# VectorE in place of GpSimd for weight splits and additions, and a smaller scratch for the distance biases, in a one-core three-layer kernel

## The chip, the core and the metric

The kernel runs on one core of a Trainium2 chip. The metric is the device time of one execution in microseconds (us): all 26 inputs lie in device memory before it starts, and the output lies there when it ends. Lower is better.

## What is computed

The input x holds 256 rows of 1024 numbers, all in fp32. Three layers run one after another; the sizes are those that matter here.

```
h = rmsnorm(x, g0); p = h @ ev_w_in (1024 x 5120)
y = concat(hgrn2_scan(...) * silu(gate), retention_scan(rope(q), rope(k), v) * silu(gate)) @ ev_w_out (1536 x 1024)
x = x + rmsnorm(y, g1);  x = x + rmsnorm(square(relu(rmsnorm(x, g2) @ w1)) @ w2, g3)      # w1 1024 x 4096, w2 4096 x 1024

h = rmsnorm(x, g0); p = h @ od_w_in (1024 x 3080)
y = (sigmoid(og) * head_rmsnorm(mlstm_scan(q, k, v, gates))) @ od_w_out (1024 x 1024)
x = x + rmsnorm(y, g1);  x = x + rmsnorm(square(relu(rmsnorm(x, g2) @ w1)) @ w2, g3)

shift, scale, gate = split(silu(c) @ w_ada + b_ada)
h = rmsnorm(x, g) * (1 + scale) + shift; q, k, v, g_attn, cb, cc, cx, g_conv, m_attn, m_conv = split(h @ w_in (1024 x 10240))
attn: softmax(q k^T / sqrt(128) + bias[head, t5_bucket(t - s)], causal) v, 8 heads of 128
y = sigmoid(m_attn) * ((attn * silu(g_attn)) @ w_o_attn) + sigmoid(m_conv) * ((cb * conv3(cc * cx) * silu(g_conv)) @ w_o_conv)
out = rmsnorm(x + gate * (y @ w_out), final_g)
```

Almost all of the arithmetic is in the products of 256 rows with the weight matrices.

## The kernel before

**Weights.** All weights are fp32 and are read once, in units of 128 x 1024 numbers (512 KB). A unit is loaded on SyncE's queue into one of five buffers `raw` (`emit_load` L359, `load` L305). `emit_split` (L375) then makes two fp32r halves of it in one of eight buffers `u`: ScalarE copies it to the high half, and the low half is the unit minus that high half, one TENSOR_TENSOR of 128x1024 on VectorE or on GpSimd. L385 to L387 choose between the two by the finishing times that the planner expects, with POOL_BIAS (L33) as a handicap for GpSimd; 19 of the 316 splits went to GpSimd. A product is three fp32r matmuls per tile, high x high, high x low and low x high (`mmA` L445 with 512 columns a matmul, `mmB` L451 with 256), so TensorE needs both halves of a unit.

**Activations.** The 256 rows are two tiles T of 128 rows. Before a product they are transposed in 128x128 blocks on TensorE (`to_act` L542, the transposes are the lines `ax<-ident,s` at L296), ScalarE copies the result to a high part `a` (`a<-ax`), and VectorE subtracts to get the low part (`a<-ax,a`).

**Order.** The program `prog` is a list of units and small functions, laid out by stage builders: `blockA` (L464), `stagA` (L481: tile T = 0 over two column blocks, then T = 1), `blockB` (L501: output transposed). `Sched` (L48) keeps an estimated clock for each engine (a ScalarE, v VectorE, g GpSimd, p TensorE) and an estimated ready time for each tile, from cost formulas such as the one in `tt` (L263). Work beside the products is written as jobs, generators that wake when the estimated clock of TensorE reaches the time at which their inputs are expected. After each unit `pump` (L395) emits loads and splits as far ahead as buffers allow; a split due later than LEAD (7000 ns) waits until L406 and L407 find the engines free. So a change of one engine's estimate moves the order of instructions on every engine. Each engine then runs its instructions in that order, waiting by semaphores.

**Between products.** At the end of a mixer or MLP, `out_stag` (L606) starts `chain` (L580) for each T: `post` (L570) computes the rms factor and twice, for halves h of 512 columns, `s<-mm,sm,s` (SCALAR_TENSOR_TENSOR, L276) and x += s, the first half on GpSimd, the second on VectorE; `pre` (L551) makes the normalised input of the next product, two L276 lines `s<-x,sm,s`, then `to_act`. In layer 3 `pre` also adds a shift (`s<-s,s`, L265 on VectorE).

**First mixer.** `rope_evac` (L880) rotates q and k: three VectorE products and an addition of 128x512 on GpSimd (L893), then transposes. `ev_first` (L723) evicts v and the gate; the gate's product with `ghg` is done by GpSimd (L736).

**Second mixer (mLSTM).** `od_gates` (L1133) ends in `spread` (L1171): the row `ig` is written to a scratch `scr_m` in device memory and read back to 128 partitions, both on SyncE's queue. `mix_out` (L1293) computes for each T and pair of heads i numerator, denominator and head norm with small operations on 128x1 and 128x2 columns (`sm`), and writes y by two L276 lines. `od_og` (L1215) multiplies y by the sigmoid of the output gate (`s<-s,s`, L265 on VectorE) and calls `to_act`; the product with od_w_out follows.

**Distance biases.** `bias_rows` (L644) computes in the first MLP, early in the kernel, one row of 384 biases per head (8 partitions), and writes it to a scratch `scr` of [8, 128, 384] in device memory, the same row 128 times, on SyncE's queue. `bias_job` (L1436) reads it in layer 3 with a row pitch of 383, so that partition p sees its row shifted by p: 128 partitions x 8 heads x 256 numbers. The loads of weights before and after stand in the same queue.

GpSimd executes 44 instructions: 19 splits, 8 additions to x, 4 of rope, 2 products with `ghg`, and 11 memsets.

Of the kernel before, what the change touches and what calls it, by code (L numbers as in the profile page):

```python
# [10 lines left out]
F32 = mybir.dt.float32  # L11
# [3 lines left out]
ALU = mybir.AluOpType  # L15
# [14 lines left out]
SPREAD = 4000.0  # L30
MARGIN = 400.0
LEAD = 7000.0
POOL_BIAS = -200.0  # L33


LAST = -1.0
# [167 lines left out]
def tile_model(ctx: ExitStack, tc: tile.TileContext, I: dict, out: bass.AP, stop=None):  # L204
    nc = tc.nc
    sc = Sched()
# [4 lines left out]
    dram = ctx.enter_context(tc.tile_pool(name="scratch", bufs=1, space=bass.MemoryType.DRAM))  # L211
# [4 lines left out]
    def nm(p):  # L216
        cnt[0] += 1
        return f"{p}{cnt[0]}"

    def a8(dt=F32):  # L220
        return pool.tile([128, 2048], dt, tag="a8", bufs=6, name=nm("a8_"))

    def s4(dt=F32, n=1024):
        return pool.tile([128, n], dt, tag="s4", bufs=10, name=nm("s4_"))

    def s2(dt=F32, n=512):
        return pool.tile([128, n], dt, tag="s2", bufs=8, name=nm("s2_"))
# [9 lines left out]
    def axb():  # L237
        t = psum.tile([128, 512], F32, tag="ax", bufs=4, name=nm("ax_"))
        sc.reuse("ax", 4, t)
        return t  # L240


    def fs(ap):
        n = 1
        for s in ap.shape[1:]:
            n *= s
        return n
# [4 lines left out]
    def A(o, i, f=AF.Copy, **kw):  # L252
        c = fs(i) / 1.2 + 90
        ptr = [kw[k] for k in ("bias", "scale") if isap(kw.get(k))]
        acc = [kw["accum_out"]] if isap(kw.get("accum_out")) else []
        c += 93 * len(ptr) + 93 * len(acc)
        if f in TABLES and TABLES[f] != sc.table:
            sc.table = TABLES[f]
            c += 1283
        sc.op("a", c, [o] + acc, [i] + ptr)  # L260
        nc.scalar.activation(o, i, f, **kw)  # L261

    def tt(o, a, b, op, e="v"):  # L263
        sc.op(e, fs(o) * (1.0417 if e == "v" else 2.1) + 70, [o], [a, b])
        (nc.vector if e == "v" else nc.gpsimd).tensor_tensor(out=o, in0=a, in1=b, op=op)  # L265
# [8 lines left out]
    def stt(o, a, s, b, op0, op1, **kw):  # L274
        sc.op("v", fs(o) * 1.0417 + 70 + (60 if isap(s) else 0), [o], [a, b] + ([s] if isap(s) else []))
        nc.vector.scalar_tensor_tensor(out=o, in0=a, scalar=s, in1=b, op0=op0, op1=op1, **kw)  # L276
# [13 lines left out]
    def mm(o, l, r, start, stop_, c):  # L290
        sc.op("p", c, [o], [l, r])
        nc.tensor.matmul(o, l, r, start=start, stop=stop_)  # L292

    def tr(o, i, idt, c=107.0):
        sc.op("p", c, [o], [i, idt])
        nc.tensor.transpose(o, i, idt)  # L296
# [4 lines left out]
    def bc(ap2, n):  # L301

        return ap2[:, None, :].to_broadcast([ap2.shape[0], n, ap2.shape[1]])

    def load(o, i, q=None):  # L305
        sc.came(o, max(sc.E["p"], 0.0) + 4000.0)
        (q or nc.sync).dma_start(o, i)


    x = cpool.tile([128, 2, D], F32, name="x")  # L310
# [48 lines left out]
    def emit_load():  # L359
        k = st["load"]  # L360
        kind, val = order[k]
        t = pool.tile([128, 1024], F32, tag="raw", bufs=RB, name=nm("raw_"))
        src = units[val] if kind == "w" else val[0]
        if len(src.shape) == 3:
            load(t.rearrange("p (a c) -> p a c", a=src.shape[1]), src)
        else:
            load(t, src)
        raws[k] = t
        free = st["done"][k - RB] if k >= RB else 0.0
        st["dma"] = max(st["dma"], free + 2000.0) + 1480.0  # L370
        st["arrive"].append(st["dma"])
        sc.W[t.tensor.name] = [(0, 1024, st["dma"], "d")]
        st["load"] += 1

    def emit_split():  # L375
        k = st["split"]
        kind, val = order[k]
        t = raws.pop(k)
        if kind == "w":
            u = pool.tile([128, 2, 1024], F32R, tag="u", bufs=NU, name=nm("u_"))  # L380
            if len(st["free"]) >= st["nu"] - NU + 1 > 0:
                sc.W[u.tensor.name] = [(0, 2048, st["free"][st["nu"] - NU], "p")]
            st["nu"] += 1
            A(u[:, 0, :], t)
            hi_t = sc.E["a"] + sc.OTHER  # L385
            fv, fg = max(sc.E["v"], hi_t) + 1137.0, max(sc.E["g"], hi_t) + 2220.0
            tt(u[:, 1, :], t, u[:, 0, :].bitcast(F32), ALU.subtract, "g" if fg < fv + POOL_BIAS else "v")  # L387
            tiles[val] = u
            st["live"] += 1
        else:  # L390
            val[1](t)
        st["done"].append(max(sc.E["v"], sc.E["a"] + 1300.0))
        st["split"] += 1

    def pump():  # L395
        while True:
            k = st["split"]
            if st["load"] < len(order) and st["load"] < k + RB:
                emit_load()
                continue  # L400
            if k >= len(order):
                return
            if order[k][0] == "w" and st["live"] >= NU:
                return
            if order[k][0] == "w" and due[order[k][1]] - st["at"] > LEAD:
                if st["arrive"][k] > sc.t + 300 or sc.E["a"] > sc.t + 800 or \  # L406
                        min(sc.E["v"], sc.E["g"] + 1100.0) > sc.t + 500:  # L407
                    return
            elif st["arrive"][k] > sc.t + 1500:
                return  # L410
            emit_split()
# [158 lines left out]
    def post(T, st_, yb, g):  # L570

        rs = st_.second(yb[1])
        for h in range(2):
            c = slice(h * 512, h * 512 + 512)
            t = s2()
            stt(t, yb[h], rs, g[:, c], ALU.mult, ALU.mult)
            tt(x[:, T, c], x[:, T, c], t, ALU.add, "g" if h == 0 else "v")
        yield

    def chain(T, st_, yb, gpost, gpre, act, shift=None):  # L580
# [53 lines left out]
    E3 = {}  # L634
# [9 lines left out]
    def bias_rows():  # L644
        oh, rb, bm = E3["oh"], E3["rb"], E3["bm"]
        pb = axb()
        mm(pb[0:8, 0:384], rb[0:32, 0:8], oh[0:32, :], True, True, 640.0)
        tt(bm[0:8, :], pb[0:8, 0:384], bm[0:8, :], ALU.add)
        yield 1000.0
        scr = E3["scr"] = dram.tile([8, 128, 384], F32, name="scr")  # L650
        load(scr, bm[0:8, None, :].to_broadcast([8, 128, 384]))
        yield LAST


# [68 lines left out]
    def ev_first(T, b, ps):  # L723
        if T == 0:
            E1["vg", b] = s4()
            if b == SMALL:
                small_loads()
        if b == 0:
            v = E1["vg", 0][:, T * 512:T * 512 + 512]
            A(v, ps)  # L730
            E1["v", T] = v
        else:
            s_ = E1["vg", 1][:, T * 512:T * 512 + 512]
            A(s_, ps, AF.Sigmoid)
            tt(s_, ps, s_, ALU.mult)
            tt(s_.rearrange("p (h c) -> p h c", h=4), s_.rearrange("p (h c) -> p h c", h=4), bc(ghg, 4),  # L736
               ALU.mult, "g")
            E1["g", T] = s_
        if T == 1 and b == 0:
            sc.start(vec_job())  # L740

    stagA([(w_ev, 1024), (w_ev, 1536)], h0.get, ev_first, h0.before)

    def ev_f(ps):
# [135 lines left out]
    def rope_evac(key):  # L880
        def evac(ps):
            def job():
                dst = s4()
                E1[key] = dst
                for T in range(2):
                    p3 = ps[T].rearrange("p (h c) -> p h c", h=4)
                    m1, m2 = s2(), s2()
                    a3, b3 = (m.rearrange("p (h c) -> p h c", h=4) for m in (m1, m2))
                    cs, sn = (E1[k][:, T * 128:T * 128 + 128] for k in ("cos", "sin"))
                    tt(a3, p3, bc(cs, 4), ALU.mult)  # L890
                    tt(b3[:, :, 0:64], p3[:, :, 64:128], bc(sn[:, 0:64], 4), ALU.mult)
                    tt(b3[:, :, 64:128], p3[:, :, 0:64], bc(sn[:, 64:128], 4), ALU.mult)
                    tt(m1, m1, m2, ALU.add, "g")  # L893
                    yield
                    pt = axb()
                    for h in range(4):
                        tr(pt[:, h * 128:h * 128 + 128], m1[:, h * 128:h * 128 + 128], ident)
                    A(dst[:, T * 512:T * 512 + 512], pt)
                yield LAST
            E1[key + "job"] = sc.start(job())  # L900
        return evac
# [436 lines left out]
    m1 = Stage()  # L1338
# [97 lines left out]
    def bias_job():  # L1436
        scr = E3["scr"]
        E3["bias"] = a8().rearrange("p (h c) -> p h c", h=8)
        load(E3["bias"], bass.AP(tensor=scr.tensor, offset=scr.offset + 127,
                                 ap=[[383, 128], [128 * 384, 8], [1, 256]]))  # L1440
        yield LAST

    def silu_fm(ps, dst):
# [338 lines left out]
```

## Time and profile before

| | |
|---|---|
| three runs | 1004.68, 1004.59, 1003.57 us; median 1004.59 |
| the profiled execution | 1004.45 us |
| span of its trace, first to last instruction | 1002.6 us, mean granted TensorE clock 0.991 |
| busy TensorE / VectorE / ScalarE / GpSimd | 974.5 / 678.7 / 540.6 / 70.8 us |
| memory traffic | 187.46 MB read, 2.63 MB written |

The profile's times are microseconds from the span's start. PE is TensorE, DVE VectorE, ACT ScalarE, POOL GpSimd, SP SyncE. L265 is line 265 of the kernel; `out<-in` names tiles without their numbers (`mm` and `ax` are PSUM banks, `s` half or full working tiles, `sm` small columns). An idle time in brackets is that of the engine just before the instruction, with what ended it. PEclk is the TensorE clock that was granted, 1.00 being 2.4 GHz and 0.50 being 1.2 GHz.

### The profile page before, as it was taken

What the parts mean: (1) busy time and instruction counts of PE and PEld (TensorE: products, weight loads), DVE (VectorE), ACT (ScalarE), POOL (GpSimd) and SP (SyncE); (2) the same over time, 40 slices, a digit from 0 to 9 for tenths busy, and PEclk for the clock granted to TensorE, in tenths of its full rate; (3) what the DMA queues carried; (4) which work ended last, traced back from release to release, by engine and by line L of the source; (5) the groups of instructions that cost most, each with busy time, mean ns of one, the idle gap of its engine ahead of it and who ended that gap; (6) DMA issues with size and microseconds to landing.
All of it is one profiled execution on the core that took longest, in us unless ns stands there. A gap on an engine that the chain in (4) does not pass through costs nothing.

```text
span 1002.6 us, 15544 instructions
## 1 busy us (share of the span) xinstructions
PE 974.5 (97%) x6168; PEld 879.6 (88%) x6168; DVE 678.7 (68%) x852; ACT 540.6 (54%) x772; POOL 70.8 (7%) x44
## 2 busy tenths in 40 slices
PE   8999999999999899997999999999999999999997
PEld 6988888789989787986789999987999999999995
DVE  6769874875553367788698778658645677447564
ACT  7753674764542366766565545546545546444533
POOL 0212200200000001101201001001000010001000
PEclk9999999999999999998999999999999999999999
DMA  8762536566765666635489988635865445665631
GB/s 313 247 219 84 169 126 189 164 193 190 231 191 104 177 216 193 200 130 183 134 284 315 339 299 275 187 86 176 289 199 160 142 127 169 215 185 175 195 113 42
DMA packets 85100, 191.09 MB, mean 191 GB/s; under 512 B 7072, under 2 KB 10400, under 8 KB 85028
## 3 DMA queue, kind: packets, MB, share of 16 engines
q1 hardware_dynamic: 84740, 189.58, 59.8%
q8 instruction: 48, 0.79, 0.3%
q10 hardware_dynamic: 288, 0.52, 0.1%
q14 instruction: 24, 0.20, 0.1%
HBM read 187.46 MB, written 2.63 MB: 190 GB/s over the span
## 4 chain that ended last, share of the span: by engine, by line
PE 41%; issue 7%; DVE 2%; POOL 0%; ACT 0%; DVEq 0%; POOLq 0%
PE mm L292 35%; PE ax L292 6%; PE ax L296 1%; DVE s L265 1%; DVE u L265 0%; DVE s L276 0%; POOL u L265 0%; DVE s L271 0%; DVE x L265 0%; ACT junk L261 0%; POOL x L265 0%; ACT s L261 0%; DVE a L265 0%; ACT u L261 0%; DVE sm L280 0%
## 5 line engine op out<-in xcount | busy, mean ns | idle before, releaser
L265 DVE TENSOR_TENSOR u<-raw,u 128x1024 fp32r<-128x1024 f32 x297 | 368.0, 1253 | 212.1 <-ACT u L261 208.7
L261 ACT ACTIVATE u<-raw 128x1024 fp32r<-128x1024 f32 x316 | 329.9, 1056 | 276.6 <-PE mm L292 142.9
L292 PE MATMUL mm<-u,a 128*128 128x512 f32 x1968 | 473.4, 396 | 4.2 <-DVE a L265 3.2
L292 PEld LDWEIGHTS mm<-u,a 128*128 128x128 f32 x1968 | 368.3, 190 | 82.4 <-DVE a L265 4.6
L292 PE MATMUL mm<-a,u 128*128 128x256 f32 x2496 | 305.3, 284 | 0.0
L292 PEld LDWEIGHTS mm<-a,u 128*128 128x128 f32 x2496 | 301.5, 192 | 0.6
L292 PE MATMUL ax<-a,u 128*128 128x256 f32 x1152 | 142.4, 285 | 3.6 <-ACT u L261 2.9
L292 PEld LDWEIGHTS ax<-a,u 128*128 128x128 f32 x1152 | 141.3, 193 | 5.0 <-ACT u L261 3.1
L265 POOL TENSOR_TENSOR u<-raw,u 128x1024 fp32r<-128x1024 f32 x19 | 47.9, 2526 | 457.9 <-ACT u L261 332.0
L280 DVE RECIPROCAL sm<-sm 128x1 f32<-128x1 f32 (+2 forms) x43 | 7.0, 163 | 53.1 <-ACT sm L261 44.4
L296 PE MATMUL ax<-ident,s 128*128 128x128 f32 (+1 forms) x196 | 30.4, 275 | 11.2 <-DVE s L265 7.3
L261 ACT ACTIVATE s<-mm 128x512 f32<-128x512 f32 x64 | 35.6, 588 | 10.4 <-PE mm L292 10.1
L296 PEld LDWEIGHTS ax<-ident,s 128*128 128x128 f32 (+1 forms) x196 | 22.7, 140 | 19.4 <-issue 6.7
L261 ACT ACTIVATE a<-s 128x512 fp32r<-128x512 f32 (+1 forms) x37 | 23.8, 644 | 28.9 <-DVE s L265 28.1
L261 ACT ACTIVATE s<-ax 128x512 f32<-128x512 f32 (+1 forms) x43 | 24.3, 566 | 25.3 <-PE ax L296 13.9
L261 ACT ACT_TABLE_LOAD x27 | 34.6, 1283 | 2.0 <-DVE lbv L265 0.9
L265 DVE TENSOR_TENSOR s<-mm,s 128x512 f32<-128x512 f32 (+1 forms) x46 | 27.7, 638 | 10.8 <-PE mm L292 6.8
L265 POOL TENSOR_TENSOR x<-x,s 128x512 f32<-128x512 f32 x8 | 10.3, 1290 | 343.7 <-DVE s L276 343.7
L261 ACT ACTIVATE a<-ax 128x512 fp32r<-128x512 f32 x38 | 22.2, 592 | 22.0 <-PE ax L296 21.4
L265 DVE TENSOR_TENSOR a<-s,a 128x512 fp32r<-128x512 f32 x36 | 24.9, 693 | 11.2 <-ACT a L261 8.4
L265 DVE TENSOR_TENSOR s<-s,s 128x512 f32<-128x512 f32 (+4 forms) x38 | 30.4, 803 | 2.6 <-ACT s L261 1.9
L292 PE MATMUL ax<-s,s 128*128 128x256 f32 (+2 forms) x156 | 30.7, 338 | 0.8 <-DVE s L276 0.8
(101 smaller groups left out, 432.8 us busy)
## 6 DMA issues: line engine op xcount, KB each, us to landing
raw<-in_mlp_w_dram SPq DMA_DIRECT2D x128, 512.0 KB
raw<-in_w_in_dram SPq DMA_DIRECT2D x80, 512.0 KB
raw<-in_ev_w_in_dram SPq DMA_DIRECT2D x40, 512.0 KB
raw<-in_od_w_in_dram SPq DMA_DIRECT2D x24, 512.0 KB
raw<-in_w_ada_dram SPq DMA_DIRECT2D x24, 512.0 KB
raw<-in_ev_w_out_dram SPq DMA_DIRECT2D x12, 512.0 KB
s<-in_norm_g_dram SPq DMA_DIRECT2D x8, 512.0 KB
raw<-in_od_w_out_dram SPq DMA_DIRECT2D x8, 512.0 KB
```

Of the source, the lines that this page charges most:

```text
L261: nc.scalar.activation(o, i, f, **kw)
L265: (nc.vector if e == "v" else nc.gpsimd).tensor_tensor(out=o, in0=a, in1=b, op=op)
L280: nc.vector.reciprocal(o, i)
L292: nc.tensor.matmul(o, l, r, start=start, stop=stop_)
L296: nc.tensor.transpose(o, i, idt)
```

## The change

Every `tensor_tensor` that could go to GpSimd goes to VectorE: the low halves of all weight splits, the first half of x += s in `post`, the rope addition and the product with `ghg`. `pump` looks at VectorE's estimate alone. The planner's estimates change with that, and so does the order. The bias scratch holds each row 16 times instead of 128 times; it is read back by eight loads, each for 16 partitions, whose offset goes back by 16 numbers from one load to the next, so that each partition gets the same numbers as before.

```diff
-POOL_BIAS = -200.0
...
             A(u[:, 0, :], t)
-            hi_t = sc.E["a"] + sc.OTHER
-            fv, fg = max(sc.E["v"], hi_t) + 1137.0, max(sc.E["g"], hi_t) + 2220.0
-            tt(u[:, 1, :], t, u[:, 0, :].bitcast(F32), ALU.subtract, "g" if fg < fv + POOL_BIAS else "v")
+            tt(u[:, 1, :], t, u[:, 0, :].bitcast(F32), ALU.subtract)
...
                 if st["arrive"][k] > sc.t + 300 or sc.E["a"] > sc.t + 800 or \
-                        min(sc.E["v"], sc.E["g"] + 1100.0) > sc.t + 500:
+                        sc.E["v"] > sc.t + 500:
                     return
...
             stt(t, yb[h], rs, g[:, c], ALU.mult, ALU.mult)
-            tt(x[:, T, c], x[:, T, c], t, ALU.add, "g" if h == 0 else "v")
+            tt(x[:, T, c], x[:, T, c], t, ALU.add)
...
-        scr = E3["scr"] = dram.tile([8, 128, 384], F32, name="scr")
-        load(scr, bm[0:8, None, :].to_broadcast([8, 128, 384]))
+        scr = E3["scr"] = dram.tile([8, 16, 384], F32, name="scr")
+        load(scr, bm[0:8, None, :].to_broadcast([8, 16, 384]))
...
             tt(s_.rearrange("p (h c) -> p h c", h=4), s_.rearrange("p (h c) -> p h c", h=4), bc(ghg, 4),
-               ALU.mult, "g")
+               ALU.mult)
...
-                    tt(m1, m1, m2, ALU.add, "g")
+                    tt(m1, m1, m2, ALU.add)
...
         E3["bias"] = a8().rearrange("p (h c) -> p h c", h=8)
-        load(E3["bias"], bass.AP(tensor=scr.tensor, offset=scr.offset + 127,
-                                 ap=[[383, 128], [128 * 384, 8], [1, 256]]))
+        for a in range(8):
+            load(E3["bias"][16 * a:16 * a + 16],
+                 bass.AP(tensor=scr.tensor, offset=scr.offset + 127 - 16 * a, ap=[[383, 16], [16 * 384, 8], [1, 256]]))
```

How the order moves is shown at two places. In it the lines of the changed kernel are numbered three lower, or one lower near the top, since lines went away; L264 is `tt`, L275 `stt` and L291 `mm` there.

**VectorE at the end of the first mixer, tile T = 0.** `s_269` and `s_270` are the two halves of the MLP's input, the rows with `a_265` are the low parts of their transposes, and each `u` row is a split. Before:

```order
L276 SCALAR_TENSOR_TENSOR s_269_1617<-x,sm_1609,s_240_1422 128x512
L276 SCALAR_TENSOR_TENSOR s_270_1619<-x,sm_1609,s_240_1422 128x512
L265 TENSOR_TENSOR u_1623<-raw_1480,u_1623 128x1024
L265 TENSOR_TENSOR u_1633<-raw_1498,u_1633 128x1024
L265 TENSOR_TENSOR a_265_1608<-ax_1650,a_264_1607 128x512
L265 TENSOR_TENSOR a_265_1608<-ax_1658,a_264_1607 128x512
```

and in the changed kernel:

```order
L275 SCALAR_TENSOR_TENSOR s_269_1620<-x,sm_1612,s_232_1402 128x512
L275 SCALAR_TENSOR_TENSOR s_270_1622<-x,sm_1612,s_232_1402 128x512
L264 TENSOR_TENSOR u_1627<-raw_1499,u_1627 128x1024
L264 TENSOR_TENSOR u_1638<-raw_1510,u_1638 128x1024
L264 TENSOR_TENSOR u_1649<-raw_1518,u_1649 128x1024
L264 TENSOR_TENSOR a_265_1611<-ax_1658,a_264_1610 128x512
L264 TENSOR_TENSOR a_265_1611<-ax_1666,a_264_1610 128x512
```

Three splits stand between the second half and the first low part where two stood; the third was GpSimd's (`u_1642` there).

**The last pair of heads in the mLSTM's output.** Here `s_630` (before) and `s_626` (changed) is y for T = 1, `sm` the columns of its second pair of heads. On VectorE before:

```order
L280 RECIPROCAL sm_4073<-sm_4072 128x2
L265 TENSOR_TENSOR sm_4073<-sm_4073 128x2
L276 SCALAR_TENSOR_TENSOR s_630_4094<-ax_4066,sm_4073,gml 128x256
L276 SCALAR_TENSOR_TENSOR s_630_4094<-mm_4069,sm_4073,gml 128x256
L265 TENSOR_TENSOR s_630_4094<-s_630_4094,s_611_4022 128x512
L265 TENSOR_TENSOR s_630_4094<-s_630_4094,s_634_4129 128x512
L265 TENSOR_TENSOR u_4143<-raw_4000,u_4143 128x1024
```

and in the changed kernel:

```order
L279 RECIPROCAL sm_4062<-sm_4061 128x2
L264 TENSOR_TENSOR sm_4062<-sm_4062 128x2
L275 SCALAR_TENSOR_TENSOR s_626_4085<-ax_4055,sm_4062,gml 128x256
L275 SCALAR_TENSOR_TENSOR s_626_4085<-mm_4058,sm_4062,gml 128x256
L264 TENSOR_TENSOR u_4113<-raw_3871,u_4113 128x1024
L264 TENSOR_TENSOR u_4124<-raw_4004,u_4124 128x1024
L264 TENSOR_TENSOR s_626_4085<-s_626_4085,s_609_4017 128x512
L264 TENSOR_TENSOR s_626_4085<-s_626_4085,s_634_4129 128x512
```

Two splits now stand ahead of the products with the gate, where one stood behind them. On TensorE, T = 0's y (`s_606` before, `s_604` in the changed kernel) is transposed a little earlier in the program. Before, the transposes of its first half stood ahead of the last pair's numerators for T = 1 (`ax_4066`, then `mm_4069`):

```order
L296 MATMUL ax_4050<-ident,s_606_3988 128x128 x4
L292 MATMUL mm_4024<-u_3762,a_488_3219 128x512
L292 MATMUL mm_4024<-u_3783,a_487_3218 128x512 x2
L292 MATMUL ax_4066<-s_522_3372,s_575_3812 128x257
```

and in the changed kernel, where the last pair's numerators are `ax_4055` and `mm_4058`:

```order
L291 MATMUL ax_4055<-s_517_3360,s_569_3793 128x257
L291 MATMUL ax_4055<-s_533_3455,s_568_3788 128x257
L291 MATMUL mm_4058<-s_517_3360,s_569_3793 128x257
L291 MATMUL mm_4058<-s_533_3455,s_568_3788 128x257
L295 MATMUL ax_4074<-ident,s_604_3983 128x128 x4
```

The transposes now stand behind the four matmuls of the numerators.

## Rows read from the trace of the kernel before

**Rows 1.** The page's first part: busy time, share of the span and instructions of each engine.

```profile
PE 974.5 (97%) x6168; PEld 879.6 (88%) x6168; DVE 678.7 (68%) x852; ACT 540.6 (54%) x772; POOL 70.8 (7%) x44
```

**Rows 2.** Timeline of PE, several windows: start, length, operation, [idle before and its releaser].

```profile
75.75 0.66 PE L296 MATMUL ax<-ident,s 128*128 128x128 f32 x4 [1.45 <-POOL s L265]
...
190.49 0.74 PE L292 MATMUL mm<-u,a 128*128 128x512 f32 x2 [1.82 <-DVE a L265]
...
341.08 0.50 PE L292 MATMUL ax<-a,u 128*128 128x256 f32 x2 [2.87 <-ACT u L261]
342.33 1.43 PE L292 MATMUL ax<-a,u 128*128 128x256 f32 x5 [0.76 <-DVE u L265]
...
456.98 0.66 PE L296 MATMUL ax<-ident,s 128*128 128x128 f32 x4 [1.96 <-DVE s L265]
...
470.58 0.63 PE L296 MATMUL ax<-ident,s 128*128 128x128 f32 x4 [3.57 <-DVE s L265]
...
679.61 0.66 PE L296 MATMUL ax<-ident,s 128*128 128x128 f32 x4 [1.73 <-DVE s L265]
```

**Rows 3.** Windows, PE's L292 alone: length, busy, busy (instructions), PEclk, DMA share, GB/s.

```profile
192.00:195.00 3.00, 3.00 (x9) 0.50 0.91 315
...
342.50:345.00 2.50, 2.50 (x12) 0.50 0.74 279
...
458.00:461.40 3.40, 3.40 (x11) 0.50 0.09 37
...
471.70:475.00 3.30, 3.30 (x8) 0.50 0.79 318
...
680.00:683.00 3.00, 2.79 (x11) 1.00 0.61 175
```

**Rows 4.** Timeline of ACT at 340, and windows of all engines while `scr` is written.

```profile
339.97 1.06 ACT L261 ACTIVATE u<-raw 128x1024 fp32r<-128x1024 f32 x1 [23.08 <-DMA raw<-in_mlp_w_dram]
...
310.00:337.90 27.90, 27.90 (x192) 26.01 (x191) 3.68 (x3) 3.18 (x3) 0.00 (x0) 1.00 0.60 102
```

**Rows 5.** DMA traffic from 308 to 337.9: packets in all.

```profile
DMA packets 1471, 2.97 MB, mean 99 GB/s; under 512 B 52, under 2 KB 1030, under 8 KB 1469
```

**Rows 6.** Timeline of POOL, two windows.

```profile
74.42 1.27 POOL L265 TENSOR_TENSOR s<-s,s 128x512 f32<-128x512 f32 x1 [2.62 <-DVE s L265]
...
185.90 2.85 POOL L265 TENSOR_TENSOR u<-raw,u 128x1024 fp32r<-128x1024 f32 x1 [4.95 <-ACT u L261]
```

**Rows 7.** Timeline of DVE, several windows.

```profile
185.27 4.56 DVE L265 TENSOR_TENSOR u<-raw,u 128x1024 fp32r<-128x1024 f32 x2
...
453.30 2.12 DVE L265 TENSOR_TENSOR sm<-sm 128x2 f32<-128x2 f32 x1
...
466.88 2.05 DVE L265 TENSOR_TENSOR sm<-sm 128x2 f32<-128x2 f32 x1
...
676.69 2.86 DVE L265 TENSOR_TENSOR s<-s,s 128x512 f32<-128x512 f32 x1
```

**Rows 8.** Lines of tiles `u` and `x`: count, duration ns min/median/max, first and last start.

```profile
L265 DVE TENSOR_TENSOR u<-raw,u x297: 1202/1225/3429, 8.3 to 974.9; 128x1024 fp32r<-128x1024 f32 x149
...
L265 DVE TENSOR_TENSOR x<-x,s x12: 691/1226/1293, 180.3 to 996.3; 128x512 f32<-128x512 f32 x12
```

**Rows 9.** Windows of all engines in the first mixer (PE, PEld, DVE, ACT, POOL).

```profile
62.00:122.00 60.00, 58.54 (x343) 49.92 (x342) 53.83 (x67) 27.50 (x32) 14.75 (x8) 1.00 0.45 144
```

**Rows 10.** Timeline of SP: the issues of the small scratches.

```profile
304.52 0.81 SPq L307 DMA_DIRECT2D scr<-s  x1
...
423.36 0.36 SPq L307 DMA_DIRECT2D scr_m<-s  x1
426.74 0.34 SPq L307 DMA_DIRECT2D s<-scr_m  x1
...
721.04 0.46 SPq L307 DMA_DIRECT2D a<-scr  x1
```

**Rows 11.** DMA traffic from 723.5 to 726.9: packets in all.

```profile
DMA packets 1158, 1.27 MB, mean 374 GB/s; under 512 B 32, under 2 KB 1056, under 8 KB 1157
```

## The prediction

> **What bounds the kernel now.** I read the busy times first, then what ended TensorE's idle times, then TensorE's clock, and last the engines it waits for. TensorE is busy for 974.5 of the 1002.6 us span, VectorE for 678.7, GpSimd for 70.8 [rows 1]. So TensorE is the bound, and its work is untouched. A change here can only give back the 28 us in which TensorE is idle, and the time in which it runs slowly. The reader should see two things. The larger idle times are few, and most end with VectorE or GpSimd at the seam between two products [rows 2]; the one at 341, of 2.87 us, ends with ScalarE's copy of a weight unit. And behind the gaps of 1.82, 2.87 + 0.76, 1.96 and 3.57 us the granted clock is 0.50, the lower of its two levels, while behind the gap of 1.73 it is 1.00 [rows 2, 3]. The stretch at 458 shows 0.50 over 3.4 us [rows 3], and work that needs 1.7 us at the full clock takes 3.4 there: a drop costs about 1.7 us on top of its gap. I use that price for all four.
>
> **Why VectorE is late at the seams.** At 185.27 two splits take 4.56 us together [rows 7]. A split takes 1.225 us in the median, and 3.429 at most [rows 8]; that maximum is the second of this pair. GpSimd runs a split from 185.90 to 188.75 [rows 6], and VectorE's op, begun inside that time, ends at 189.83, a split's own length later: it stood still until then. The operations on two columns at 453.30 and 466.88 take 2.12 and 2.05 us instead of the 0.16 or so of their kind, and the shift addition at 676.69 takes 2.86 [rows 7] against the 0.691 that an addition of this size needs at the least [rows 8]. So a VectorE operation that reads two operands beside a running GpSimd operation is held until that one ends. The change takes GpSimd's operations away; VectorE gets their work.
>
> **What VectorE gets.** 19 splits of 1.225 us, and 14 operations of 128x512 of 0.69 us: 23.3 + 9.7 = 33 us on an engine with 324 us to spare. In the trace it loses holds of 2.2 (185.27), 1.95 (453.30), 1.9 (466.88) and 2.2 us (676.69), and 0.5 us in the median for the second addition to x (1.226 against 0.691) [rows 7, 8].
>
> **The sum**, against the profiled execution's own 1004.45 us (the median of the three runs, 1004.59, is the same within 0.14):
>
> 1. *Scratch write.* SP issues it at 304.52 [rows 10]. From 308 to 337.9 the trace counts 1030 packets under 2 KB, the scratch's 1536-byte rows [rows 5], at 0.60 of DMA share for 102 GB/s [rows 4], and weights creep in beside them. ScalarE has no unit to copy for 23.08 us [rows 4]; the stock in the `u` buffers carries TensorE for about 20 of these, and the gaps of 2.87 and 0.76 follow, with a clock drop [rows 2, 3]. An eighth of 1024 packets at the same pace (1024 in some 30 us) takes 3.8 us, well inside the stock. Gain 2.87 + 0.76 + 1.7 = **5.3**. Only a pace eight times worse per packet would spoil it.
>
> 2. *First mixer to MLP, 190.49.* Instead of splits of 1.2 and 3.4 us, three of 1.13 (their pitch when they follow each other: 4.56 less 3.43) stand ahead of the low part `a`: 3.4 instead of 4.5. The gap of 1.82 shrinks by 1.1 to 0.7 and, by the gap of 1.73 that had none, brings no clock drop. Gain 1.1 + 1.7 = **2.8**; bounds 0 (a split more, holds unchanged) and 3.5.
>
> 3. *Rope, 75.75.* TensorE waits 1.45 us for GpSimd's addition [rows 2], which took 1.27 us [rows 6]; VectorE takes 0.69 and needs no handover, but may have other work in hand. I take **1.0**, bounds 0 and 1.45.
>
> 4. *mLSTM output, 456.98 and 470.58.* Two holds, 1.95 and 1.9 us, go. At the first place the order puts the numerators' four matmuls ahead of the transposes, so that TensorE has work while y is finished: gap 1.96 and drop gone, **3.7**. At the second, two splits (2.3 us) now stand ahead of the gate products where one stood behind them, which eats the hold's 1.9, and the splits are needed soon. I keep its 3.57 and its drop: 0. Bounds for both: a gain of 0.5 (the wait only moves) and of 8.9 (1.96 + 3.57 + 2 x 1.7).
>
> 5. *Second MLP to layer 3, 679.61.* The hold at 676.69 was 2.2 us and the gap 1.73: all of it goes, **1.7**; bounds 0, if a split takes the place, and 1.7.
>
> 6. *Additions to x.* Now in one line on VectorE: two products with 0.75 and two additions of 0.69. Before, the second addition was held until GpSimd's was done. The end is the same within 0.3 us: 0.
>
> 7. *New waits.* Where VectorE is nearly full the added splits come later. In 62 to 122 it is busy for 53.83 of 60 us, and GpSimd for 14.75 [rows 9]; four splits and four rope additions there are 4 x 1.13 + 4 x 0.61 = 7.0 us, and the same stretch holds eight GpSimd operations whose holds go. It fits, narrowly. In layer 3 a split may be late by a fraction. I put **-0.5** for all such places; bounds 0 and -3.
>
> 8. *Eight loads for one.* The one load was issued at 721.04 in 0.46 us [rows 10]; its packets, 1 KB each, are among the 1056 under 2 KB that landed from 723.5 to 726.9 [rows 11]. Eight issues cost 3.7 us of SP, 3.2 more than now, and the loads of weights behind them start that much later. The same stock that covered 20 us at 320 [rows 4] covers this. 0. The bound from above is the scratch of the mLSTM: write and read, one behind the other, took 3.4 us a step [rows 10]; eight such steps in a row would be 27 us, 7 beyond the cover.
>
> The Trainium skill speaks against this edit: by "SBUF — State Buffer", section "Door 1: The DMA port swizzle", 16 neighbouring partitions reach four of sixteen DMA ports, at 104 GB/s measured for 1 MiB. By that page, as an estimate, 1 MB in such pieces takes 10 us if one load runs after another, and the weights would be set back by some 7; that too lies under the cover, and the sum would not change. No row of before shows a load of 16 partitions.
>
> 5.3 + 2.8 + 1.0 + 3.7 + 1.7 - 0.5 = 14.0, so **990.5 us**.
>
> **Rivals.**
> (a) *All seams close.* The second mLSTM gap goes with its drop (5.3 more), the rest of the gap at 190 and of the rope wait too (0.7 + 0.5), and there are no new waits (0.5): 983.5. For it: every one of these waits ends with VectorE or GpSimd. Against: the two splits ahead of the gate products.
> (b) *The holds only move.* The scratch gives its 5.3, and one seam 1.7; elsewhere the splits that GpSimd did beside VectorE now stand in VectorE's line ahead of the same operation: 997.4. For it: at 190 one of three splits is exactly that.
> (c) *VectorE becomes the bound, slower.* The decisive point is 62 to 122: if the long operations there are long by themselves, not held, 53.83 + 7.0 is over 60, and every later weight half is late. Then 7 us come on top there, 2.3 for the two splits at 470, and a new gap with its drop, say 1.5 + 1.7, at 190; with the scratch's 5.3 that is 12.5 - 5.3 = 7.2 slower, 1011.7. Against it: POOL is active in nearly every long operation that I read.
> (d) *Eight loads in series.* 27 - 20 = 7 us of wait, and the drop behind it, 1.7, with the trickle of weights meanwhile another 3: 990.5 + 12 = 1002.5. Nothing in the program makes a load wait for the one before, so this is unlikely.
> (e) *The scratch write stays long*, if its time is set by its eight source partitions and not by its packets: 990.5 + 5.3 = 995.8. Against it: the packets arrive evenly over the 30 us.
>
> **How the numbers follow.** Forecast with its bounds (986 to 996) 0.71, (a) 0.08, (b) 0.12, (c) 0.03, (d) 0.03, (e) 0.03. A measurement of this kernel tells about 0.2%, or 2 us, from no change. (c) is slower; (d) falls half on faster and half on no change. That gives faster 0.95, same 0.02, slower 0.03. The range 984 to 998 takes in the forecast's case, (b), (e) and most of (a).
>
> **What would show it.** GpSimd busy for about 4 us, memsets alone; the splits' maximum near 1.25 us and the additions to x at 0.69; no ScalarE idle time of 23 us around 320, and the scratch's packets gone within 5 us; no TensorE gap at 341; a gap under 1 us at the first mixer's end, and PEclk 1.00 behind it; none at the second MLP's end; one gap of 2 to 4 us in the mLSTM's output, with 0.50 behind it. I would be wrong if VectorE's operations beside nothing on GpSimd were still long, if TensorE waited for splits (`mm<-u` or `ax<-a,u` released by DVE `u`) in several stretches, or if weights came late behind the eight loads at about 710.

## The result, and the profile after

The changed kernel takes 987.76 us in the median of four runs (986.43 to 989.62), against 1004.63 us: a ratio of 0.9835, 95% interval 0.9817 to 0.9853, which is 16.6 us less (14.8 to 18.4). The forecast was 990.5.

The profiled execution took 986.43 us, 18.0 less than that of before. The page's first part after the change:

```profile
PE 967.7 (98%) x6168; PEld 874.6 (89%) x6168; DVE 669.8 (68%) x885; ACT 541.1 (55%) x772; POOL 4.1 (0%) x11
```

The span is 984.6 us, so TensorE is idle for 16.9 us instead of 28.1 [rows 1]: 11.2 us. And the same 6168 matmuls are busy for 967.7 us instead of 974.5: 6.8 us, which go with the clock, granted at 0.999 in the mean instead of 0.991. The two make the 18.0. VectorE does 33 more operations and is busy for 9 us *less*.

TensorE's timeline at the places of [rows 2]; 341, 457 and 75.75 have no row here, since no idle time is left at 74 to 77, at 330 to 345, or ahead of the first transposes of y. The row at 479.93, at the start of the second MLP, is no place of [rows 2]; the kernel before waits there for 1.35 us:

```profile
187.86 2.34 PE L291 MATMUL mm<-u,a 128*128 128x512 f32 x9 [1.03 <-DVE a L264]
...
457.70 1.17 PE L295 MATMUL ax<-ident,s 128*128 128x128 f32 x8 [2.87 <-DVE s L264]
...
479.93 0.73 PE L291 MATMUL mm<-u,a 128*128 128x512 f32 x2 [1.07 <-ACT a L260]
...
677.83 0.66 PE L295 MATMUL ax<-ident,s 128*128 128x128 f32 x4 [0.33 <-DVE s L264]
```

The gap of 1.82 is 1.03, that of 1.73 is 0.33, and of the two in the mLSTM's output one is left, 2.87 for 3.57. The granted clock behind the gaps (windows, PE's L291 alone, columns as in [rows 3]):

```profile
187.00:190.00 3.00, 2.14 (x9) 1.00 0.91 313
...
458.00:461.00 3.00, 2.38 (x10) 1.00 1.02 327
461.00:464.00 3.00, 3.00 (x15) 1.00 0.96 307
```

In this execution it is at its upper level, 2.4 GHz, even behind the 2.87 us. Why VectorE is earlier shows in its timeline at the end of the first mixer and in the mLSTM's output, and in the lines of `u` and `x`:

```profile
183.72 3.49 DVE L264 TENSOR_TENSOR u<-raw,u 128x1024 fp32r<-128x1024 f32 x3
187.12 1.28 DVE L264 TENSOR_TENSOR a<-ax,a 128x512 fp32r<-128x512 f32 x2
...
453.62 0.16 DVE L264 TENSOR_TENSOR sm<-sm 128x2 f32<-128x2 f32 x1
...
454.61 2.35 DVE L264 TENSOR_TENSOR u<-raw,u 128x1024 fp32r<-128x1024 f32 x2
456.87 1.28 DVE L264 TENSOR_TENSOR s<-s,s 128x512 f32<-128x512 f32 x2
...
L264 DVE TENSOR_TENSOR u<-raw,u x316: 1190/1225/1228, 8.8 to 961.7; 128x1024 fp32r<-128x1024 f32 x158
...
L264 DVE TENSOR_TENSOR x<-x,s x20: 691/692/694, 177.9 to 978.5; 128x512 f32<-128x512 f32 x20
```

Three splits take 3.49 us where two took 4.56; the operation on two columns takes 0.16 where it took 2.05 [rows 7]; the slowest split is 1.228 us where it was 3.429 [rows 8]. No hold (a VectorE operation that stands still beside one of GpSimd) is left. In the row at 454.61 the reader sees what keeps the last gap: two splits ahead of the two gate products.

Four more readings: the window of all engines at 62 to 122 (columns as in [rows 9]), that of PE alone at 335 to 345, the packets of the DMA traffic from 706 to 713.2, when the eight loads of the biases ran, and their issues on SP:

```profile
62.00:122.00 60.00, 60.00 (x349) 51.52 (x349) 52.34 (x75) 26.52 (x33) 0.00 (x0) 1.00 0.34 106
...
335.00:345.00 10.00, 10.00 (x53) 1.00 0.51 155
...
DMA packets 1278, 1.34 MB, mean 186 GB/s; under 512 B 139, under 2 KB 1125, under 8 KB 1277
...
703.99 7.69 SPq L306 DMA_DIRECT2D a<-scr  x8
```

VectorE has eight more operations in 62 to 122 and is busy for 52.34 us where it was 53.83 [rows 9]; TensorE is never idle there, nor at 335 to 345. The eight loads' packets took some 7 us where the one load took 3.4 [rows 11], and SP's eight issues stretched over 7.69 us, not 3.7 (the eighth came 3.9 us behind the seventh; why is not shown). In ScalarE's timeline a single wait ends with one of these loads:

```profile
712.75 1.06 ACT L260 ACTIVATE u<-raw 128x1024 fp32r<-128x1024 f32 x1 [1.82 <-DMA a<-scr]
```

The copy ahead of it, at 709.87, waited for the same 1.82 us, for TensorE, so ScalarE lost nothing, and TensorE has no gap near it. The Trainium skill's figure for 16 partitions ("SBUF — State Buffer", "Door 1: The DMA port swizzle") gave 10 us as an estimate for loads one after another; the trace's 7 lies between that and the 3.4 of the one load. Whether the partitions or the late last issue set it, no run here shows.

### The profile page after: what moved, and what is told of

The parts are those of the page before. It is cut to its first block, busy times and chain, and to the rows that moved or that the text cites. A ratio compares the mean times of both kernels' runs of the same rounds, so it can differ in the third digit from the quotient of the medians.

```text
span 984.6 us, 15496 instructions
## 1 busy us (share of the span) xinstructions
PE 967.7 (98%) x6168; PEld 874.6 (89%) x6168; DVE 669.8 (68%) x885; ACT 541.1 (55%) x772; POOL 4.1 (0%) x11
## 4 chain that ended last, share of the span: by engine, by line
PE 86%; DVE 7%; ACT 3%; issue 2%; DMA 2%; SPq 0%; DVEq 0%; ACTq 0%
PE mm L291 66%; PE ax L291 19%; DVE u L264 3%; DVE s L275 2%; PE ax L295 2%; DMA x<-in_x_dram 1%; ACT junk L260 1%; DMA raw<-in_mlp_w_dram 1%; DVE s L264 1%; DVE x L264 1%; ACT u L260 0%; SPq L306 0%; ACT s L260 0%; ACT L260 0%; DVE a L264 0%
## 5 line engine op out<-in xcount | busy, mean ns | idle before, releaser
L264 DVE TENSOR_TENSOR u<-raw,u 128x1024 fp32r<-128x1024 f32 x316 | 380.4, 1222 | 195.4 <-ACT u L260 194.2
L291 PE MATMUL mm<-u,a 128*128 128x512 f32 x1968 | 469.3, 394 | 4.5 <-ACT a L260 2.0
L291 PEld LDWEIGHTS mm<-u,a 128*128 128x128 f32 x1968 | 364.7, 188 | 83.1 <-DVE a L264 3.5
L291 PE MATMUL mm<-a,u 128*128 128x256 f32 x2496 | 305.3, 284 | 0.0
L291 PEld LDWEIGHTS mm<-a,u 128*128 128x128 f32 x2496 | 301.5, 192 | 0.6
L291 PEld LDWEIGHTS ax<-a,u 128*128 128x128 f32 x1152 | 139.9, 192 | 0.9
L291 PE MATMUL ax<-a,u 128*128 128x256 f32 x1152 | 140.6, 283 | 0.0
L264 DVE TENSOR_TENSOR s<-mm,s 128x512 f32<-128x512 f32 (+1 forms) x46 | 27.8, 637 | 12.0 <-PE mm L291 7.7
L264 DVE TENSOR_TENSOR a<-s,a 128x512 fp32r<-128x512 f32 x36 | 24.9, 692 | 11.3 <-ACT a L260 8.8
L264 DVE TENSOR_TENSOR s<-s,s 128x512 f32<-128x512 f32 (+4 forms) x42 | 28.9, 691 | 2.8 <-ACT s L260 2.0
L264 DVE TENSOR_TENSOR a<-ax,a 128x512 fp32r<-128x512 f32 x38 | 25.6, 686 | 7.1 <-ACT a L260 7.1
L291 PE MATMUL ax<-s,s 128*128 128x256 f32 (+2 forms) x156 | 29.9, 331 | 0.0
L275 DVE SCALAR_TENSOR_TENSOR s<-raw,silc,s 128x1024 f32<-128x1024 f32 x21 | 26.9, 1279 | 0.0
```

## The experiments

Times are medians of four or five runs, beside the kernel before on the same chip, which took 1003.16 us for the runs e1, e2, e5 and e6, 1003.34 for e3, e4, e7 and e8, and 1002.73 for e9 to e11. Ratios are to that.

### The two parts apart

e1 is the kernel before with the scratch's edit alone:

```diff
-        scr = E3["scr"] = dram.tile([8, 128, 384], F32, name="scr")
+        scr = E3["scr"] = dram.tile([8, 16, 384], F32, name="scr")
...
-        load(E3["bias"], ...)
+        for a in range(8):
+            load(E3["bias"][16 * a:16 * a + 16], ...)
```

> The kernel before with the scratch part of the change alone: 16 copies, eight loads; GpSimd keeps its splits and additions. Theory (the write of 1024 packets starves the weights, the gaps of 2.87 and 0.76 and one clock drop follow): the gap at 341 goes, the gaps at 75.75, 190, 457, 470 and 679 stay as they are, time 1004.6 - 5.3 = 999.3 (998 to 1000.5). Rival (ScalarE's 23 us without units is slack, the gap at 341 comes from the order of the work): 1004.6 within 1. Rival (eight loads cost time): over 1000 with a wait for weights near 720.

Measured: 997.02 us, ratio 0.9944 (0.9927 to 0.996), a gain of 5.6 us (4.0 to 7.3), a little more than expected. The gap at 341 is gone; the others stand as they were. In its profiled execution TensorE's timeline and the clock (columns as above) read

```profile
191.24 0.96 PE L292 MATMUL mm<-u,a 128*128 128x512 f32 x3 [1.83 <-DVE a L265]
...
450.20 0.65 PE L296 MATMUL ax<-ident,s 128*128 128x128 f32 x4 [1.97 <-DVE s L265]
...
462.14 0.76 PE L296 MATMUL ax<-ident,s 128*128 128x128 f32 x4 [3.56 <-DVE s L265]
...
191.50:194.50 3.00, 3.00 (x14) 1.00 0.95 324
450.50:453.50 3.00, 2.89 (x13) 1.00 0.33 134
462.50:465.50 3.00, 2.44 (x5) 0.50 1.03 311
```

The same gaps of 1.83 and 1.97 us, untouched by this edit, here bring no clock drop, where they did in [rows 3]. Only the 3.56 did.

e2 is the changed kernel with the scratch of before (the diff of e1 the other way round, on the changed kernel).

> The changed kernel with the scratch of 128 copies and one load back: only the engine part of the change. Theory (the two parts are independent): 987.8 + 5.3 = 993 (991.5 to 994.5), with a gap of 2.9 to 3.6 near 335, ended by ScalarE's or VectorE's part of a weight unit, and PEclk 0.50 behind it; the seams as in the changed kernel. Rival (the engine part gave all, the scratch nothing): 988. Rival (the scratch gave nearly all): over 1000.

Measured: 995.8 us, ratio 0.9929 (0.9908 to 0.9949), a gain of 7.1 us (5.1 to 9.2), so somewhat slower than the 991.5 to 994.5 expected. The gap is back, with ScalarE's wait and a clock drop, here a longer one: the granted clock is 0.50 in the whole window 335 to 340 and still 0.86 in 340 to 345.

```profile
335.46 0.79 PE L291 MATMUL ax<-a,u 128*128 128x256 f32 x2 [3.56 <-ACT u L260]
336.72 1.65 PE L291 MATMUL ax<-a,u 128*128 128x256 f32 x6 [0.47 <-DVE u L264]
...
334.36 1.06 ACT L260 ACTIVATE u<-raw 128x1024 fp32r<-128x1024 f32 x1 [23.77 <-DMA raw<-in_mlp_w_dram]
...
336.00:339.00 3.00, 2.53 (x12) 0.50 0.70 251
```

Both parts are worth several microseconds. Apart they give 5.6 + 7.1 = 12.7, together 16.6; the intervals of the three are up to 2 us wide on either side. TensorE's idle times in the profiles do add up: 28.1 us before, 994.2 - 969.4 = 24.8 in e1, 992.3 - 971.4 = 20.9 in e2, 16.9 with both, so 3.3 + 7.2 against 11.2. TensorE's busy time, 974.5, 969.4, 971.4 and 967.7, gives 5.1 + 3.1 against 6.8. So the profiled executions do add up, 8.4 + 10.3 against 18.0; it is the medians that do not, and the mean granted clocks of the runs go with that. They are 0.991 to 0.994 before, 0.994 to 0.997 in e1, 0.994 to 0.999 with both, but in the three other runs of e2 0.989 to 0.992, no higher than before. Why e2's clock stayed low is not shown.

### How long a trickle the stock covers

While the scratch is written, few weights come in (the trickle), and TensorE lives on the units that are already split (the stock). e8 is the changed kernel with 64 copies and two loads of 64 partitions each:

```diff
-        scr = E3["scr"] = dram.tile([8, 16, 384], F32, name="scr")
+        scr = E3["scr"] = dram.tile([8, 64, 384], F32, name="scr")
...
-        for a in range(8):
-            load(E3["bias"][16 * a:16 * a + 16], ...)
+        for a in range(2):
+            load(E3["bias"][64 * a:64 * a + 64], ...)
```

> The changed kernel with 64 copies of a row and two loads of 64 partitions each: 512 packets. Theory (the stock of split units covers about 20 us): the packets take some 15 us, ScalarE idles 8 to 12 us longer than now for units, TensorE has no gap near 335, time 987.8 within 1.5. Rival (any long trickle costs in proportion): half of the 5.3 us, 990.5, with a gap near 325.

Measured: 987.91 us, ratio 0.9846 (0.9825 to 0.9867), as the changed kernel. ScalarE waits once for

```profile
317.77 1.06 ACT L260 ACTIVATE u<-raw 128x1024 fp32r<-128x1024 f32 x1 [7.96 <-DMA raw<-in_mlp_w_dram]
```

and TensorE has no gap over 0.25 us between 190 and 380. So the write's cost is not in proportion to its packets: 512, four times those of the changed kernel, are still free, while 1024 cost 5.6 us on the kernel before (e1) and 8 to 9 us on the changed one (e2). Where between the two the cost sets in was not measured.

### What on GpSimd costs: splits or additions

e3 puts the planner's choice of engine for the splits back into the changed kernel, and nothing else:

```diff
+POOL_BIAS = -200.0
...
-            tt(u[:, 1, :], t, u[:, 0, :].bitcast(F32), ALU.subtract)
+            hi_t = sc.E["a"] + sc.OTHER
+            fv, fg = max(sc.E["v"], hi_t) + 1137.0, max(sc.E["g"], hi_t) + 2220.0
+            tt(u[:, 1, :], t, u[:, 0, :].bitcast(F32), ALU.subtract, "g" if fg < fv + POOL_BIAS else "v")
...
-                        sc.E["v"] > sc.t + 500:
+                        min(sc.E["v"], sc.E["g"] + 1100.0) > sc.t + 500:
```

> The changed kernel with the planner's choice of GpSimd for splits put back as before; the additions to x, rope's additions and the gate products stay on VectorE, the scratch stays small. With GpSimd's estimate otherwise free the planner gives it 32 splits. Theory (a split beside VectorE's two-operand work is what costs): holds of about 2 us appear again, two to four of them at seams; TensorE's gaps grow by 3 to 9 us, time 991 to 998. Rival (the additions on GpSimd were the cost): 987.8 within 1.5.

Measured: 1010.92 us, ratio 1.0077 (1.0052 to 1.0102): slower than the kernel before, in spite of the small scratch, and well beyond what was expected. GpSimd, with no additions to do, gets 32 splits, six of them between 70 and 104 us in the first mixer, where the kernel before had two. There the timelines of GpSimd, VectorE and TensorE read

```profile
76.11 2.40 POOL L265 TENSOR_TENSOR u<-raw,u 128x1024 fp32r<-128x1024 f32 x1 [3.48 <-ACT u L261]
78.77 3.04 POOL L265 TENSOR_TENSOR u<-raw,u 128x1024 fp32r<-128x1024 f32 x1 [0.26 <-ACT u L261]
...
77.07 2.52 DVE L265 TENSOR_TENSOR s<-s,a 128x1024 f32<-128x1024 f32 x1
79.51 3.57 DVE L265 TENSOR_TENSOR a<-a 128x512 f32<-128x512 f32 x2
83.00 1.34 DVE L265 TENSOR_TENSOR s<-mm,s 128x512 f32<-128x512 f32 x3
...
85.22 1.03 PE L296 MATMUL ax<-ident,s 128*128 128x128 f32 x4 [3.12 <-DVE s L265]
```

VectorE's two operations of the scan take 2.52 and 3.57 us beside the two splits; rope's products stand behind them, and TensorE waits 3.12 us for rope's result. (In the changed kernel the same pair took 1.21 and 1.41.)

e4 puts only the additions back, the splits stay on VectorE:

```diff
-            tt(x[:, T, c], x[:, T, c], t, ALU.add)
+            tt(x[:, T, c], x[:, T, c], t, ALU.add, "g" if h == 0 else "v")
...
-               ALU.mult)
+               ALU.mult, "g")
...
-                    tt(m1, m1, m2, ALU.add)
+                    tt(m1, m1, m2, ALU.add, "g")
```

> The changed kernel with the 14 operations of 128x512 back on GpSimd (8 additions to x, 4 of rope, 2 gate products), all splits on VectorE, the scratch small. Theory: the wait of 1.45 for rope's addition returns, the second addition to x is held by 0.5 us each time, which is the same end of the chain as on VectorE alone; TensorE's gaps grow by 1 to 3 us, time 988.5 to 991. Rival (the additions were the cost): 993 or more.

Measured: 986.01 us, ratio 0.9829 (0.9808 to 0.985): no slower than the changed kernel. The wait for rope's addition did not come back:

```profile
72.36 1.28 POOL L264 TENSOR_TENSOR s<-s,s 128x512 f32<-128x512 f32 x1 [33.26 <-DVE s L264]
...
73.75 0.63 PE L291 MATMUL mm<-u,a 128*128 128x512 f32 x2
74.21 0.60 PE L295 MATMUL ax<-ident,s 128*128 128x128 f32 x4
```

GpSimd's 1.28 us lie there as in [rows 6], and TensorE does not wait. What had been late before was VectorE, held by a split on GpSimd just ahead, as its trace shows:

```profile
69.33 2.48 POOL L265 TENSOR_TENSOR u<-raw,u 128x1024 fp32r<-128x1024 f32 x1 [28.42 <-ACT u L261]
69.47 3.61 DVE L265 TENSOR_TENSOR a<-a 128x512 f32<-128x512 f32 x2
```

In e4 the same pair of `a<-a` starts at 69.54 and takes 1.41 us. So of the engine part the splits are the whole gain: e1 and e4 differ in the splits alone, and in the order that follows from them, and lie at 0.9944 and 0.9829, 11.5 us apart. Moving the 14 additions gives nothing that these runs can tell.

### The hold by itself

e5 adds to the changed kernel, in `pre` behind the second half of the normalised input, a GpSimd operation whose result nobody reads; e6 puts one small operation and four memsets there instead:

```diff
...
+        hb3 = hb[1][:, None, 0:416].to_broadcast([128, 2, 416])
+        nc.gpsimd.tensor_tensor(out=st["side"].rearrange("p (a c) -> p a c", a=2), in0=hb3, in1=hb3, op=ALU.subtract)
```

> The changed kernel plus ten GpSimd operations whose result nobody reads: at each norm ahead of a product, as soon as the second half of the normalised input stands, a TENSOR_TENSOR of 128x832 that reads SBUF, about 1.95 us by the share of the split's 2.4. Theory (a VectorE operation with two SBUF operands is held until GpSimd's ends): the splits or shift additions behind the norm take up to 1.9 us longer, the gaps at the seams grow by 0.5 to 1.9 each at five or more of the eight seams, some with clock drops; 5 to 14 us more in all, 993 to 1002. Rival (the gain came from the order and the handovers between engines, GpSimd beside VectorE costs nothing): 987.8 within 1.5, no VectorE operation longer than alone.

```diff
...
+        nc.gpsimd.tensor_tensor(out=st["tiny"], in0=hb[1][:, 0:16], in1=hb[1][:, 0:16], op=ALU.subtract)
+        for i in range(4):
+            nc.gpsimd.memset(st["side"], 0.0)
```

> The same places, but GpSimd does one TENSOR_TENSOR of 128x16 and then four memsets of 128x416, about 1.8 us that read nothing. Theory (what holds VectorE is GpSimd reading SBUF beside it): splits and additions keep 1.22 and 0.69 us but for the first moment, time 987.8 within 1.5. Rival (any GpSimd operation holds VectorE): as in the run with reads, 993 to 1002.

Measured: e5 995.73 us, ratio 0.9923 (0.9908 to 0.9937); e6 986.43 us, ratio 0.9837 (0.982 to 0.9853). At the end of the first mixer GpSimd and VectorE show, in e5,

```profile
185.42 2.42 POOL L565 TENSOR_TENSOR side<-s 128x832 bf16<-128x832 f32 x1 [162.84 <-DVE s L275]
...
185.19 4.87 DVE L264 TENSOR_TENSOR u<-raw,u 128x1024 fp32r<-128x1024 f32 x3
...
190.71 1.66 PE L291 MATMUL mm<-u,a 128*128 128x512 f32 x6 [2.40 <-DVE a L264]
```

and in e6

```profile
184.16 1.13 POOL L565 TENSOR_TENSOR tiny<-s 128x16 f32<-128x16 f32 x1 [160.88 <-DVE s L275]
185.23 1.95 POOL L567 MEMSET side<- 128x416 f32 x4
...
184.00 3.51 DVE L264 TENSOR_TENSOR u<-raw,u 128x1024 fp32r<-128x1024 f32 x3
```

Beside the reading operation the three splits take 4.87 us, 1.4 more than the 3.49 of the changed kernel, and the gap grows by as much, from 1.03 to 2.40. Beside 1.95 us of memsets they take 3.51. Nothing else was changed in either, the order of VectorE's work least of all. So it is shown that a GpSimd operation that reads SBUF holds VectorE's splits, that one which only writes does not, and that the hold reaches TensorE at a seam. It goes both ways: the small operation of 128x16 lasts 1.13 us here in e6, where VectorE's first split had begun before it, and 0.21 us where the shortest of its ten ran. That is the lock of the Trainium skill's page "SBUF — State Buffer", section "SBUF: two separate sides": whoever of the two starts first has the shared port for its whole operation. The rows agree.

The price in time is e5's 995.73 against the changed kernel's 987.76: ten operations on an engine that nobody waits for cost 8 to 9 us (by the ratios 8.8), and the same ten places with memsets nothing. How much of the change's own gain comes from the holds and how much from the new order of instructions, these runs do not divide.

### A version that beats both

The last large gap, 2.87 us, stands in TensorE's order: T = 1's transposes of y come ahead of matmuls for T = 0 whose splits are there. e7 has the two jobs that emit them yield longer:

```diff
             tt(y, y, sg, ALU.mult)
-            yield
+            yield ((8500.0, 5500.0)[b] if T == 1 else 0.0)
```

> The changed kernel with T = 1's transposes of the mLSTM's y emitted later (two jobs yield for 8.5 and 5.5 us of the planner's time), so that on TensorE 12 and 15 matmuls of the next product, 2.6 us and more, stand ahead of them instead of none. Theory (the gap of 2.87 us at 454.8 is an order that asks for y too early, the work to fill it is there): the gap shrinks below 0.6, no clock drop there in any execution, time 987.8 - 2.5 = 985.3, less up to 1 for drops that some executions had (984 to 986). Rival (the wait moves to the start of T = 1, which needs these transposes): 987 to 989, a new gap of 1.5 to 3 us near 460.

Measured: 982.97 us, ratio 0.98 (0.9776 to 0.9824), all four runs between 982.71 and 983.72, so better than expected. The timeline of TensorE now reads

```profile
451.68 5.60 PE L291 MATMUL mm<-u,a 128*128 128x512 f32 x24
457.42 0.63 PE L295 MATMUL ax<-ident,s 128*128 128x128 f32 x4
457.80 0.94 PE L291 MATMUL mm<-u,a 128*128 128x512 f32 x3
```

The transposes start at nearly the same time as in the changed kernel, 457.42 for 457.70, and the wait is filled. Two more runs add the additions on GpSimd to this, and a third repeats e7 beside them:

> The two best in one: the 14 operations of 128x512 on GpSimd, all splits on VectorE, the scratch small, and T = 1's transposes of y later. Theory (the two do not touch each other: 6.6 us of gaps over 250 ns with the additions on GpSimd, of which 2.86 was this wait): gaps of about 4 us in all, time 982.0 (981 to 983). Rival (what the additions on GpSimd hold of VectorE comes out once the large gap no longer covers it): 983.5 or more.

> Only the 8 first halves of x += s on GpSimd; rope, gate product and all splits on VectorE, scratch small, transposes of y later. Theory (the additions to x end at the same time on either side): 982.5 (981.5 to 983.7), as the kernel with all on VectorE and the transposes later. Rival (a held second addition of 1.29 us moves the seams): 984 to 986, the seams' gaps over 1.5.

> The kernel with the later transposes once more, beside the two others on one chip: 983.0 (982.3 to 983.8), no gap over 1.1 us.

Measured: e9 983.09 us, ratio 0.9805 (0.9787 to 0.9823); e10 982.92, 0.98 (0.9782 to 0.9818); e11, the same kernel as e7, 984.34, 0.9816 (0.9799 to 0.9833). e9 missed its 981 to 983 by a little and e11 its 982.3 to 983.8. The intervals of the three overlap, though on their one chip e11's five runs (983.67 to 984.72) lie a little above e10's four (981.94 to 983.83). So where the additions run matters by 1 to 2 us at most, and the order of the transposes is worth some 2 to 3.5 us over the changed kernel's ratio of 0.9835.

## Why the prediction was right, and where it was not

The direction and the two main mechanisms, the starved weights and the holds, held: 14.0 us were forecast, 16.6 measured, 987.76 within 984 to 998. Rope's cause and the price of the clock did not. By its steps:

1. *Scratch write, 5.3.* Right for the kernel before: e1 gives 5.6 (on the changed kernel, e2 shows 8 to 9), and e2 and e8 show the cause: with 128 copies ScalarE starves and TensorE has its gap, with 64 it waits for 8 us and TensorE has none.
2. *End of the first mixer, 2.8.* Right but for 0.3: the gap shrank to 1.03, not to 0.7, and the clock stayed up (in e1's profile it did so behind the whole 1.83, so this 1.7 is not sure).
3. *Rope, 1.0.* The size was near (1.45, the whole wait), the cause wrong. I put the wait down to GpSimd's addition, since that released TensorE. e4 has the addition on GpSimd and no wait. It was late because VectorE's scan, held by a split on GpSimd, was late ahead of it.
4. *mLSTM output, 3.7.* The step that was mis-sized. The first gap went, as said. Of the second I wrote "I keep its 3.57 and its drop: 0"; it came out at 2.87, and without a drop in the profiled execution. That execution lies 4.0 us below the forecast: 2.3 in idle times (11.2 for 8.9), of which 0.7 are here, 0.45 at rope and the rest in small gaps, and 1.7 in the clock (6.8 for 5.1). In the median the forecast fell short by 2.6.
5. *Second MLP to layer 3, 1.7.* A gap of 0.33 is left: 1.4.
6. *Additions to x, 0.* Right, shown by e4, e9 and e10.
7. *New waits, -0.5.* VectorE had room: 52.34 of 60 us in the fullest stretch. New gaps of about 0.4 at 18.9 and 491 stand against old ones of about 0.8 that shrank to 0.3. Nearly 0.
8. *Eight loads, 0.* Right: twice as slow in transfer, with issues over 7.69 us for the 3.7 of the sum, and covered.

Of the rivals, (c), VectorE as the bound, is out: the long operations of [rows 7] were holds, as e5 and e6 show. (b), holds that only move, is out by the gaps that went, (d), loads in series, by TensorE's having no gap near 712, and (e), a write that stays long, by e1. (a), with all seams closed, was half true: the clock came back in full in the profiled execution, the 2.87 stayed until e7 filled it.

What was wrong in the method is the fixed price of 1.7 us for a clock drop behind each of four gaps. The profile of before holds a fifth stretch at the lower level, in the window 10 to 15, which the forecast left out. So the 6.8 us of busy time between before and after are five drops, 1.4 each; e1, with one drop, is busy 1.7 us longer than the changed kernel. And that a gap of some length brings a drop is not certain, as the last section shows.

## What to carry to other kernels

Where GpSimd helps VectorE with elementwise work on SBUF, look for VectorE operations that last as long as GpSimd's beside them: 33 operations on GpSimd, most of its 70.8 us, left VectorE busy for 9 us more than without that help. Put the help where VectorE is not on the way to the next matmul, or leave it out. A replicated write through DMA in small rows was free here as long as the stock of prepared weights outlasted it (512 packets) and cost 5.6 us or more when it did not (1024); and a wait that is left may be an order that asks too early, which here a move of eight transposes cured.

## What was not expected of the hardware

The clock's drop behind a gap is not a function of the gap's length alone. One and the same wait, of 2.84 to 2.87 us ahead of T = 1's transposes, stands in six profiles: the clock stayed at 1.00 in the changed kernel, e2, e4 and e6, and fell in e5 and e8. In e8:

```profile
457.76 1.94 PE L295 MATMUL ax<-ident,s 128*128 128x128 f32 x8 [2.87 <-DVE s L264]
...
459.00:461.00 2.00, 1.65 (x5) 0.61 0.67 209
```

The gaps of 1.82 and 1.96 us had a drop before and none in e1; that of 2.40 in e5 had none. All gaps of 3.56 and 3.57 (before, e1, e2, e3) had one; behind the first 20 us none of those under 1.8 did. The first matmuls of the kernel show the same chance: in the window 10 to 15 the clock was 0.66 before and in e8, and 1.00 in the changed kernel (windows, PE alone; before, then changed):

```profile
10.00:15.00 5.00, 4.90 (x15) 0.66 1.03 397
...
10.00:15.00 5.00, 4.81 (x18) 1.00 1.03 383
```

Single executions of one kernel differ with their clock: the changed kernel's four runs, 986.43, 987.38, 988.15 and 989.62 us, have mean granted clocks of 0.999, 0.997, 0.997 and 0.994. The kernel of e7, with no gap over 1.03 us behind the first 17, has the narrowest times. What decides between drop and no drop behind equal gaps these runs do not show.
